# New durations for TensorE in the build-time account that orders a two-block transformer kernel

## The chip, the cores and the metric

The kernel runs on one core of one Trainium2 chip. The time is that of one execution on the device, in microseconds (us), from the first to the last instruction as the runs report it. The profile is of one such execution; its engines are called PE (TensorE, matrix products), PEld (its weight loads), DVE (VectorE), ACT (ScalarE), POOL (GpSimd) and SP (SyncE, which starts most transfers).

## The reference, cut to what matters

Two blocks of two layers each, over 256 tokens of width 1024, all in float32. The first block has a mixing layer with three kinds of heads and a SwiGLU; the second block has a gated linear recurrence (a), differential attention (b), a Fourier branch (c) and a merge of the three.

```
def _mixing(h, w_in, ...):                       # first block
    p = h @ w_in
    qa, ka, va, qi, ki, wi, qb, kb, vb, qc, kc, vc = split(p)
    qa, ka, qc, kc = rope(rms(.));  qi, ki = rope(.)
    oa = _dsa(qa, ka, va, qi, ki, wi)            # top 64 keys by an index score, then softmax
    ob = _stick_breaking(qb, kb, vb)             # cumulative sums over the keys
    oc = _swa_sinks(qc, kc, vc, sinks)           # band of 128 keys, softmax with sinks
    return rms(concat(oa, ob, oc), g_out) @ w_o

for l in range(2):
    sh1, sc1, g1, sh2, sc2, g2 = split(silu(c) @ w_mod[l] + b_mod[l])
    h = rms(x, ln1[l]) * (1 + sc1) + sh1
    x = x + g1 * _mixing(h, ...)
    h = rms(x, ln2[l]) * (1 + sc2) + sh2
    x = x + g2 * ((silu(h @ w_gate) * (h @ w_up)) @ w_down)

for l in range(2):                               # second block, with a context of 256 more tokens
    h = rmsnorm(x) * (1 + scale) + shift;  hc = rmsnorm(ctx) * (1 + scale_c) + shift_c
    aq, ak, av, ag, ao, az, bq, bk, bv, bz, cu, cz, mg = split(h @ w_in)     # and the same of hc
    y_a = rmsnorm(mlstm(aq, ak, av, ag)) * sigmoid(ao) * silu(az)
    y_b = rmsnorm(attend(bq, bk, bv, lam)) * silu(bz)
    y_c = real(fft2(cu)) * silu(cz)
    x = x + gate * (sum(sigmoid(mg_i) * (y_i @ w_i_out)) @ w_out)            # ctx likewise in layer 0
```

## The kernel before

All weights pass through SBUF once, in blocks of up to 8 x 128 rows and 256 columns. SP fetches a block into one of two buffers `raw`; ACT casts it to a float32r part `whi`, and DVE or POOL subtracts to get the rest `wlo`. The activations are split in the same way (`hhi` and `hlo`, or two planes of `h`). A dense product is three float32r matmuls per 128 rows (hi times hi, hi times lo, lo times hi): `mm3`, `dense_t` and `dense_n`. Some 24 of these 256-column matmuls make one group, and after each group the program calls `tick`.

Everything else is written between the groups. Each attention stage is a Python generator, an item of the class `Pipe`, that yields what its next piece reads. `tick` does four things: it may write one step of the modulations, a product of 32 rows by 512 columns over a fetched tile of weights `gw` (`fill`, `gemv`; such a step shows as x4 in the program's order and as x8 in the trace); it splits part of a weight block (`split_half`); it fetches (`ahead`); and it calls `Pipe.step`, which writes the next piece of each item that is ready. `drain` does the same without dense products until given items are finished. The weight blocks, gw tiles, PSUM banks and scratch tiles are rings, so that a piece that is written earlier also claims its buffers earlier.

What is ready is decided while the program is written, by `Clock`: an account of the time at which each engine gets to what it has been given. `Clock.run` starts an instruction at the latest of its engine's time, its inputs' and its ring's, and doubles a cost on PE where the account holds the clock to be low. `Engine.cost` gives the durations and `Engine.__getattr__` enters every instruction that the program writes; since it is also the helper that issues the real instruction, nearly every row of the trace has its line, L160. `Pipe.ready` lets a piece be written when its inputs' time is no later than PE's time in the account plus a slack; `fill_time`, `spare_time`, `ahead` and `split_half` compare with PE's time too. So the account sets the order in which each engine's queue is written, and nothing else: every engine works through its queue in that order, and waits are semaphores.

Names that the rows below show: `RC` are the rotated queries and keys of the c heads, `PC`, `PA` and `kk` projections, `aT` and `cT` their transposes, `S` scores, `nmax` the negative row maxima, `zB` and `eB` the stick-breaking logits and their sums, `rs` and `sst` a reciprocal root by three Newton steps on POOL; in the second block `M` and `wT` are masked weights of the recurrence and their transposes, `hA` its output, `rr` and `sh` its norm, `rsB` and `rtB` the norms of the b heads, `y` and `oB` normed head outputs. `stick`, `turned`, `attend` and `squares` in `mixing` write the first block's pieces; `tile_` and `out` in `a_items` and `b_items` the second's.

Of the kernel before, what the change touches and what calls it, by code (L numbers as in the profile page):

```python
# [7 lines left out]
F32 = mybir.dt.float32  # L8
# [17 lines left out]
EPS = 1e-6  # L26

# columns of w_in
QA, KA, VA, QI, KI, WI, QB, VB = 0, 256, 320, 384, 640, 704, 708, 1220
# columns of w_in_2  # L30
# [9 lines left out]
class Nothing:  # L40
    """stands for every object of a dry pass over the program"""
# [24 lines left out]
class Clock:  # L66
    """A rough account, while the program is written down, of when each engine gets to what it is given, in
    microseconds. Only the order in which independent work is written rests on it."""
# [20 lines left out]
    def cold(self):  # L89
        """whether the tensor engine's clock would slow down after this window of time"""  # L90
        return self.work.get(int(self.t["pe"] / 3.41), 0) < 3060

    def run(self, engine, outs, ins, cost, columns=0, delay=0.0):
        t = max([self.t[engine], self.ready(ins) + LAT] + [self.free.get(o.name, 0.0) + LAT for o in outs])
        if engine == "pe":
            w = int(t / 3.41)
            if self.work.get(w - 1, 0) < 3060:                      # the clock at half its rate
                cost *= 2
            self.work[w] = self.work.get(w, 0) + columns
# [15 lines left out]
def rows(aps):  # L115
    return aps[0].shape[0] / 128


class Engine:
# [3 lines left out]
    def cost(self, fn, out, ins, k):  # L123
        size = lambda ap: math.prod(ap.shape[1:])
        n = size(out)
        if self.name == "pe":
            if fn == "transpose":
                return 0.107, n * rows(ins)
            f = 1 if k["rhs"].dtype == F32R else 4
            c = max(0.107, n * f / 2400)  # L130
# [12 lines left out]
    def __getattr__(self, fn):  # L143
        real = getattr(self.real, fn)

        def call(*a, **k):
# [11 lines left out]
            else:  # L158
                self.clock.run(self.name, outs, aps, *self.cost(fn, outs[0], aps, k))
# [10 lines left out]
class Pool:  # L170
# [18 lines left out]
    def free(self, tag, bufs):  # L189
        """when the next place of a ring of tiles is free"""  # L190
# [9 lines left out]
def prm(ph):  # L200
    """the parameters of a phase: NAME_ph or NAME"""
# [8 lines left out]
class Pipe:  # L210
    """Work in stages beside the dense products. An item is a generator that yields what its next stage reads first. Each
    step writes the next stage of the items under way for which that is ready by the clock and starts new ones; of a
    group, limit items are under way at once."""
# [9 lines left out]
    def add(self, gen, after=(), group=None, limit=0, rank=5):  # L223
        """those of a lower rank come first"""
# [49 lines left out]
    def needed(self, items):  # L274
        """what has to run for items to finish"""
# [16 lines left out]
class Program:  # L292
    def __init__(self, tc, stack, args, out, order=None, upto=None):
# [8 lines left out]
        self.every, self.nticks = 0, 0         # a step of the modulations after every so many ticks  # L302
        self.pending = []
        self.nd = self.ns = self.nt = 0        # blocks fetched, split, taken
        self.hold = True                       # no blocks yet
        self.gd = self.gt = 0                  # rows for the modulations fetched, taken
# [18 lines left out]
    def any_ps(self):  # L325
        """a bank where nothing but dense products runs"""
# [9 lines left out]
    # =====================================================================================  # L336
    # Weights: blocks of up to 8 x 128 rows and 256 columns in the order of their use, fetched ahead and split
    # exactly into two float32r parts. A block: (rows of 128, ((tensor, layer, first row, first column, n), ...)).
    # The modulations' weights come apart from them, 128 rows at a time: (tensor, layer, first row, first column, n).
    # =====================================================================================  # L340
# [25 lines left out]
    def split_half(self, now=True):  # L366
        """splits one half of the next block's rows; False when there is nothing to do (if not now: nothing that has
        come by the clock)"""
# [24 lines left out]
    def ahead(self, g=0, n=0):  # L393
        """fetches what has a free place by the clock, and at least the first g rows and n blocks"""
# [21 lines left out]
    def drop(self, back=0):  # L416
        """the block taken last (or before) is used up"""
# [1621 lines left out]
```

## Time and profile before

| | |
|---|---|
| time, median of 3 runs | 2404.87 us (2397.66 to 2409.1) |
| profiled execution, span | 2406.6 us |
| PE busy | 2275.1 us, 95% of the span |
| DVE, ACT, POOL busy | 54%, 43%, 16% |
| mean granted clock of PE | 0.960 of full |
| bytes moved | 350.62 MB, mean 146 GB/s |

The profiled execution has no time of its own beside its span; the span lies 1.7 us above the median of the runs and inside their range. PE works through one queue in order, so time is lost where a piece at the head of that queue waits for another engine, and where PE runs at a lower granted clock. The program runs through the first block's layer 0 (mixing to about 210 us, SwiGLU to 440), its layer 1 (to 660 and 850), the second block's layer 0 (heads to 1320, merge to 1780) and layer 1 (heads to 2160, merge to the end).

### The profile page before, as it was taken

Reading aid. Unit: us, or ns where it says so; the run is one execution under the profiler, and the core shown is the slowest. Engines: PE = TensorE matmul, PEld = TensorE weight load, DVE = VectorE, ACT = ScalarE, POOL = GpSimd, SP = SyncE. Lnnn points to the kernel's source line nnn. Section 1 sums busy time; section 2 is a strip of 40 time slices with the busy share of each in tenths; the row PEclk is TensorE's granted clock in tenths of the full one; section 3 lists DMA queues with packets and bytes.
Section 4 is the critical chain, followed back from the end, with each engine's and each line's share of the span. In section 5 each row is a group of like instructions: output and inputs, shape, how many; then the busy total and the mean of one; then the engine's idle time right before and its main releaser. Section 6 shows DMA issues by size and latency. Waiting matters only on the chain. (4 is left out here: it accounts for less than half of the span.)

```text
span 2406.6 us, 39016 instructions
## 1 busy us (share of the span) xinstructions
PE 2275.1 (95%) x15672; PEld 2001.2 (83%) x15672; DVE 1298.5 (54%) x2556; ACT 1028.4 (43%) x1983; POOL 377.6 (16%) x901
## 2 busy tenths in 40 slices
PE   5988999898799999999799999999999999999999
PEld 2876889776689988888688888888897998889999
DVE  2745555675455546566564424435354665655665
ACT  2543435445344435555454323323254455544543
POOL 2321001452100001230232000000011332230000
PEclk8969999997899999999999999999999999999999
DMA  8727896652687542221222534433342322237765
GB/s 279 229 102 230 265 287 222 191 192 93 191 268 227 185 130 62 80 71 61 74 88 83 146 91 118 108 105 105 105 141 75 97 89 77 92 119 206 206 178 160
DMA packets 397142, 350.62 MB, mean 146 GB/s; under 512 B 12801, under 2 KB 366465, under 8 KB 396449
## 3 DMA queue, kind: packets, MB, share of 16 engines
q1 hardware_dynamic: 386752, 321.29, 44.2%
q0 software_dynamic: 8768, 23.76, 3.2%
q10 hardware_dynamic: 1440, 3.08, 0.4%
q8 instruction: 123, 2.02, 0.4%
q14 instruction: 59, 0.48, 0.1%
HBM read 335.50 MB, written 10.49 MB: 144 GB/s over the span
## 5 line engine op out<-in xcount | busy, mean ns | idle before, releaser
L160 DVE TENSOR_TENSOR wlo<-raw,whi 128x1024 fp32r<-128x1024 f32 (+1 forms) x465 | 548.7, 1213 | 439.7 <-ACT whi L160 438.6
L160 ACT CAST whi<-raw 128x1024 fp32r<-128x1024 f32 (+3 forms) x476 | 471.2, 1031 | 219.1 <-PE ps_mm L160 68.8
L160 PE MATMUL ps_mm<-whi,h 128*128 128x256 f32 x2304 | 442.2, 289 | 11.5 <-ACT h L160 4.5
L160 PEld LDWEIGHTS ps_mm<-whi,h 128*128 128x128 f32 x2304 | 364.2, 191 | 35.6 <-issue 17.6
L160 PE MATMUL ps_mm<-wlo,h 128*128 128x256 f32 x1152 | 324.1, 281 | 2.5 <-DVE wlo L160 2.5
L160 PE MATMUL ps_mm<-h,whi 128*128 128x512 f32 (+2 forms) x912 | 237.2, 349 | 0.0
L160 PEld LDWEIGHTS ps_mm<-wlo,h 128*128 128x128 f32 x1152 | 220.6, 191 | 6.6 <-DVE wlo L160 2.9
L160 PEld LDWEIGHTS ps_mm<-h,whi 128*128 128x128 f32 (+1 forms) x912 | 154.5, 185 | 32.6 <-issue 8.0
L160 PE MATMUL ps_mm<-h,wlo 128*128 128x512 f32 (+2 forms) x456 | 158.2, 347 | 0.0
L160 PE MATMUL ps_t<-h,whi 128*128 128x512 f32 (+1 forms) x592 | 147.9, 340 | 0.0
L160 PE MATMUL ps_s<-h,whi 128*128 128x256 f32 (+1 forms) x576 | 138.8, 332 | 0.0
L160 PE MATMUL ps_mm<-hhi,whi 128*128 128x256 f32 x416 | 124.5, 299 | 7.8 <-DVE xT L160 7.8
L160 PE MATMUL ps_mm<-hhi,wlo 128*128 128x256 f32 x416 | 120.9, 291 | 2.0 <-POOL wlo L160 2.0
L160 PE MATMUL ps_g<-gw,c 128*32 128x512 f32 (+1 forms) x640 | 97.4, 611 | 26.0 <-DMA gw<-in_w_mod_dram 18.6
L160 PE MATMUL ps_mm<-hlo,whi 128*128 128x256 f32 x416 | 121.0, 291 | 0.0
L160 PEld LDWEIGHTS ps_t<-h,whi 128*128 128x128 f32 x592 | 101.6, 188 | 12.6
L160 ACT ACTIVATE M<-ps_s,nmB,rsB 128x512 f32<-128x512 f32 (+1 forms) x96 | 67.0, 702 | 93.8 <-DVE nmB L160 93.8
L160 PEld LDWEIGHTS ps_s<-h,whi 128*128 128x128 f32 x576 | 97.5, 188 | 10.8
L160 PE MATMUL ps_t<-h,wlo 128*128 128x512 f32 (+1 forms) x296 | 100.8, 340 | 0.0
L160 PEld LDWEIGHTS ps_mm<-hhi,whi 128*128 128x128 f32 x416 | 83.0, 199 | 21.0 <-DVE xT L160 11.1
L160 PE MATMUL ps_s<-h,wlo 128*128 128x256 f32 (+1 forms) x288 | 96.0, 333 | 0.1
L160 PEld LDWEIGHTS ps_mm<-h,wlo 128*128 128x128 f32 (+1 forms) x456 | 84.5, 185 | 13.3 <-DVE wlo L160 0.2
(429 smaller groups left out, 5129.0 us busy)
## 6 DMA issues: line engine op xcount, KB each, us to landing
raw<-in_w_in_dram SPq DMA_DIRECT2D x72, 1024.0 KB, 5.2
raw<-in_w_in_dram SPq DMA_DIRECT2D x100, 512.0 KB, 4.2
gw<-in_w_mod_dram SPq DMA_DIRECT2D x96, 512.0 KB, 5.5
gw<-in_w_ada_dram SPq DMA_DIRECT2D x64, 384.0 KB, 5.4
raw<-in_w_gate_dram SPq DMA_DIRECT2D x44, 512.0 KB, 4.1
raw<-in_w_up_dram SPq DMA_DIRECT2D x44, 512.0 KB, 5.5
raw<-in_w_down_dram SPq DMA_DIRECT2D x16, 1024.0 KB, 5.0
raw<-in_w_out_dram SPq DMA_DIRECT2D x12, 1024.0 KB, 5.1
```

The costliest lines, as they stand in the source:

```text
L160: return real(*a, **k)
```

## The change

The costs of PE in the account change, and results of PE count as made 0.12 us after the engine is done with them. In `Engine.cost`, a transpose goes from 0.107 to 0.110 us; a float32r matmul of n columns from max(0.107, n/2400) to max(0.110, n/2400 + 0.014), which is 0.1207 in place of 0.107 for 256 columns and 0.2273 in place of 0.2133 for 512; a float32 matmul from max(0.107, 4n/2400) to two passes of max(0.107, n/1200) with 0.005 on top, three quarters of it where the operand has fewer than 128 rows. No instruction is added or taken away: PE has 15672 before and after.

```diff
@@ Engine.cost
         if self.name == "pe":
             if fn == "transpose":
-                return 0.107, n * rows(ins)
-            f = 1 if k["rhs"].dtype == F32R else 4
-            c = max(0.107, n * f / 2400)
+                return 0.110, n * rows(ins)
+            if k["rhs"].dtype == F32R:
+                return max(0.110, n / 2400 + 0.014), n * rows(ins)
+            c = 2 * max(0.107, n / 1200) + 0.005
+            if rows(ins) < 1:
+                c *= 0.75
             return (c / 3 if "tile_position" in k else c), n * rows(ins)
@@ Engine.__getattr__
-                self.clock.run(self.name, outs, aps, *self.cost(fn, outs[0], aps, k))
+                self.clock.run(self.name, outs, aps, *self.cost(fn, outs[0], aps, k), delay=0.12 if self.name == "pe" else 0.0)
...
```

The rest of the diff takes out comments. The helper's line is L163 in the changed kernel. Most of the order stays; what moves, moves by one group of 24 dense matmuls in most places. Three places follow. A row gives the line, the operation, out<-in, the size and how many stand together.

PE's queue at the end of the first block's layer 0 mixing, where the dense products of `w_in` have run out and `drain` writes the rest; before:

```order
L160 MATMUL ps_t<-ident,kk 128x128 x2
L160 MATMUL ps_g<-gw,c_88 32x512 x4
L160 MATMUL ps_t<-ident,RC 128x128 x2
L160 MATMUL ps_o<-PC,zB 128x64 x4
L160 MATMUL ps_t<-ident,PA 128x128 x4
L160 MATMUL ps_t<-ident,RC 128x128 x4
L160 MATMUL ps_s<-aT 128x256 x4
L160 MATMUL ps_s<-aT 128x128 x4
L160 MATMUL ps_t<-ident,RC 128x128 x4
L160 MATMUL ps_o<-PC,zB 128x64 x8
L160 MATMUL ps_t<-ident,S 128x128 x8
L160 MATMUL ps_s<-cT 128x256 x4
```

and the same place after:

```order
L163 MATMUL ps_t<-ident,kk 128x128 x2
L163 MATMUL ps_t<-ident,RC 128x128 x2
L163 MATMUL ps_t<-ident,PA 128x128 x4
L163 MATMUL ps_t<-ident,RC 128x128 x4
L163 MATMUL ps_o<-PC,zB 128x64 x12
L163 MATMUL ps_t<-ident,RC 128x128 x4
L163 MATMUL ps_s<-aT 128x256 x4
L163 MATMUL ps_s<-aT 128x128 x4
L163 MATMUL ps_s<-cT 128x256 x4
L163 MATMUL ps_t<-ident,S 128x128 x8
L163 MATMUL ps_g<-gw,c_88 32x512 x4
L163 MATMUL ps_o<-PA,S 128x64 x8
```

The modulation step behind `kk` has gone to a place behind the first eight transposes of `S`; all twelve products with `zB` and both groups of `RC` now stand ahead of the scores, and the first scores with `cT` ahead of the transposes of `S`. Further up, the stick-breaking scores and their sums are each written one group of 24 earlier; further down, the end of the stage holds four steps of the modulations (x4 + x4 + x8) where it held five.

PE's queue at the end of the a heads in the second block's layer 0 (each "..." is a group of 24 dense matmuls); before:

```order
L160 MATMUL ps_t<-ident,M_11533 128x128 x4
...
L160 MATMUL ps_o<-av,wT 128x256 x4
L160 MATMUL ps_t<-ident,M_11602 128x128 x2
L160 MATMUL ps_o<-av,wT 128x256 x2
L160 MATMUL ps_t<-ident,hA 128x128 x8
L160 MATMUL ps_mm<-whi_11741,h_6167 128x256
```

and after:

```order
L163 MATMUL ps_o<-av,wT 128x256 x4
L163 MATMUL ps_t<-ident,M_11581 128x128 x2
...
L163 MATMUL ps_o<-av,wT 128x256 x2
...
L163 MATMUL ps_t<-ident,hA 128x128 x8
L163 MATMUL ps_mm<-whi_11770,h_6167 128x256
```

The last pieces of the a heads stand one and two groups earlier, so 48 dense matmuls now lie between the last transposes of `M` and those of `hA`; the number of dense matmuls ahead of `hA` is the same. POOL's queue at this place keeps its order: two chains `rsB`, then `sh` and `rr`.

PE's queue at the end of the first block's layer 1 mixing; before:

```order
L160 MATMUL ps_o<-PA,S 128x64 x12
L160 MATMUL ps_g<-gw,c_88 32x512 x4
L160 MATMUL ps_t<-ident,PC 128x128 x8
L160 MATMUL ps_s<-eB,masks_253 128x256
...
L160 MATMUL ps_t<-ident,PA 128x128 x4
...
L160 MATMUL ps_g<-gw,c_88 32x512 x12
```

and after:

```order
L163 MATMUL ps_o<-PA,S 128x64 x12
L163 MATMUL ps_t<-ident,PC 128x128 x8
...
L163 MATMUL ps_s<-eB,masks_253 128x256
...
L163 MATMUL ps_t<-ident,PA 128x128 x4
...
L163 MATMUL ps_g<-gw,c_88 32x512 x16
```

The modulation step ahead of the transposes of `PC` is gone from there and stands as a fourth step at the end; the first "..." after is 12 dense matmuls that now lie between those transposes and the sums over `eB`. SP writes the first blocks of `w_gate` and `w_up` one step of the modulations earlier, behind four gw tiles in place of six.

## Rows read from the trace of the kernel before

**Rows 1.** Windows by stage: us, busy PE, PEld, DVE, ACT, POOL; granted clock, DMA

```profile
50.00:210.00 160.00, 147.48 (x968) 120.86 (x969) 90.58 (x247) 73.02 (x160) 42.89 (x83) 0.86 0.56 182
440.00:660.00 220.00, 185.94 (x1212) 154.16 (x1212) 123.47 (x313) 92.87 (x194) 77.75 (x116) 0.83 0.52 165
850.00:1320.00 470.00, 441.19 (x3170) 389.93 (x3169) 273.59 (x684) 227.59 (x572) 93.19 (x307) 0.97 0.25 78
1780.00:2160.00 380.00, 360.81 (x2679) 326.90 (x2678) 223.95 (x492) 184.03 (x394) 104.99 (x307) 0.98 0.32 97
```

**Rows 2.** Timeline, PE, end of layer 0's mixing: start, duration, operation [idle before <- releaser]

```profile
124.36 0.28 PE L160 MATMUL ps_mm<-wlo,hhi 128*128 128x256 f32 x1
124.48 0.28 PE L160 MATMUL ps_mm<-whi,hlo 128*128 128x256 f32 x1
...
126.61 1.00 PE L160 MATMUL ps_o<-PC,zB 128*128 128x64 f32 x8
...
132.76 1.12 PE L160 MATMUL ps_t<-ident,RC 128*128 128x128 f32 x4 [4.70 <-POOL RC L160]
...
137.72 1.52 PE L160 MATMUL ps_s<-aT 64*128 64x128 f32 x8 [1.83 <-DVE nmax L160]
...
174.17 1.94 PE L160 MATMUL ps_g<-gw,c 128*32 128x512 f32 x8
...
178.01 1.06 PE L160 MATMUL ps_g<-gw,c 128*32 128x512 f32 x8
...
185.50 1.05 PE L160 MATMUL ps_g<-gw,c 128*32 128x512 f32 x4 [1.86 <-DMA gw<-in_w_mod_dram]
```

**Rows 3.** Timeline, DVE and POOL, what the wait for RC comes from

```profile
111.66 1.02 DVE L160 SCALAR_TENSOR_TENSOR zB<-ps_s,zB 128x512 f32<-128x512 f32 x2 [1.34 <-PE ps_s L160]
...
119.75 0.21 POOL L160 TENSOR_SCALAR rs<-ss 128x16 int32<-128x16 int32 x1 [4.90 <-DVE ss L160]
...
131.44 1.26 POOL L160 TENSOR_TENSOR RC<-RC,rope_t 128x512 f32<-128x512 f32 x1
```

**Rows 4.** Window in that stage, columns as in rows 1

```profile
140.00:176.00 36.00, 36.00 (x144) 29.85 (x143) 9.84 (x49) 17.64 (x63) 0.00 (x0) 0.50 0.00 1
```

**Rows 5.** Timeline, PE and DVE, end of the first block's layer 1 mixing

```profile
575.65 1.94 PE L160 MATMUL ps_g<-gw,c 128*32 128x512 f32 x8
...
576.82 0.95 DVE L160 SCALAR_TENSOR_TENSOR eB<-zB,eB 128x768 f32<-128x768 f32 x1
...
580.67 1.11 PE L160 MATMUL ps_t<-ident,PC 128*128 128x128 f32 x4 [2.04 <-DVE hlo L160]
...
616.52 1.08 PE L160 MATMUL ps_g<-gw,c 128*32 128x512 f32 x4 [2.45 <-DMA gw<-in_w_mod_dram]
617.76 1.92 PE L160 MATMUL ps_g<-gw,c 128*32 128x512 f32 x4 [0.16 <-DMA gw<-in_w_mod_dram]
```

**Rows 6.** Timeline, POOL, DVE and PE, end of the a heads

```profile
1150.52 1.30 POOL L160 TENSOR_TENSOR rtB<-rsB 128x16 f32<-128x16 f32 x1
1150.52 2.37 DVE L160 TENSOR_TENSOR wlo<-raw,whi 128x1024 fp32r<-128x1024 f32 x2 [0.66 <-ACT whi L160]
1153.65 0.21 POOL L160 TENSOR_TENSOR rtB<-rsB 128x16 f32<-128x16 f32 x1
1159.66 0.20 POOL L160 TENSOR_TENSOR rr<-rr,rt 128x4 f32<-128x4 f32 x1
1160.40 2.03 PE L160 MATMUL ps_t<-ident,hA 128*128 128x128 f32 x8 [11.19 <-DVE hA L160]
```

**Rows 7.** Waits of PE, 1780 to 2160 us: total, times, longest

```profile
PE ps_mm L160 <- ACT whi L160: 3.2, 2, 1.9
PE ps_t L160 <- DVE y L160: 2.9, 5, 1.0
```

**Rows 8.** One round of the a heads: DVE makes M, PE transposes it

```profile
918.45 0.35 DVE L160 SCALAR_TENSOR_TENSOR M<-M,den,M 128x128 f32<-128x128 f32 x1
921.49 0.60 PE L160 MATMUL ps_t<-ident,M 128*128 128x128 f32 x4
```

## The prediction

> **What bounds the kernel now.** I read the windows by stage first, because PE's share of the whole says nothing about where its queue stands still. In [rows 1] the span less PE's busy time is 160 - 147.48 = 12.5 us in the first layer's mixing, 220 - 185.94 = 34.1 in the second's, 470 - 441.19 = 28.8 in the heads of the second block's layer 0 and 380 - 360.81 = 19.2 in those of its layer 1: 94.6 of the 131.5 us that PE is idle in all (2406.6 - 2275.1). The clock column says more of the first two: 0.86 and 0.83. So the kernel is bound by PE's queue, and what an order can give back lies in these four stages: waits at the head of the queue, and time at the lower clock. Then I read the timelines of the places where the two orders differ, asking at each which producer ends last.
>
> At the end of layer 0's mixing PE waits 4.70 us for POOL's RC and 1.83 for the maxima on DVE [rows 2]. Behind that it is busy all 36.00 of 36 us at a granted clock of 0.50, the lower of the two levels, 1.2 GHz [rows 4]. At the end of the a heads it waits 11.19 us for hA [rows 6], the longest wait of those stages.
>
> **The change, part by part.** Nothing is added or removed. The account now charges a group of 24 dense 256-column matmuls 24 x 0.1207 = 2.90 us in place of 24 x 0.107 = 2.57. In the trace their starts lie 124.48 - 124.36 = 0.12 us apart, or 24 x 0.12 = 2.88 [rows 2], so the account comes close. What follows is that inputs look ready fewer matmuls later: pieces move by whole groups, about 2.88 us of cover each, and modulation steps move where their turn falls.
>
> End of layer 0's mixing. (a) The stick-breaking scores and sums stand one group earlier. They feed DVE's zB, which feeds its next operations, then the sums of squares, POOL's root and POOL's RC: DVE waits 1.34 us for PE there, POOL 4.90 us for DVE's ss, and RC ends at 131.44 + 1.26 = 132.70 [rows 3], 0.06 before PE resumes. The bounds are 0 and -2.88; I take -1.3, the wait of DVE that goes away, since ahead of it DVE is at work. (b) All zB products and both groups of RC now stand ahead of the scores. The 1.83 us wait for the maxima is filled with that work: -1.83, with bounds 0 and -1.83. (c) The eight zB matmuls of 1.00 us lose their cover, since they ran before the wait on RC and now run behind it: +1.0. (d) The modulation step behind kk ran free, inside the same wait. Of the five steps, the one free step is gone, the two single ones in the tail are now both where PE is at the lower clock, so 2 x 1.94 in place of 1.94 + 1.06, or +0.88, and one goes to w_o, where dense work follows, at +1.06. (e) With the earlier steps sooner, their gw places come free sooner, and the last step's wait for its DMA goes: -1.86 (bounds 0 and -1.86). The sum for this stage is -1.3 - 1.83 + 1.0 + 0.88 + 1.06 - 1.86 = -2.05. What is late next is the softmax of the first group, for which the scores with cT are now the cover.
>
> End of layer 1's mixing [rows 5]. The step at 575.65 goes (-1.94). The wait of 2.04 us for hlo goes, because hlo is now written ahead of the work on eB on DVE, whose first operation started at 576.82; the sums over eB come late instead, by about the 0.95 us of such an operation, with twelve dense matmuls as cover: -2.04 + 0.95. The step comes back at the end as a fourth in a row that lives on DMA: the last one in the trace takes 617.76 + 1.92 - 616.52 = 3.16 us with its two tiles, beside a wait of 2.45 before it. SP also puts the first blocks of w_gate and w_up ahead of two of its tiles. So +3.16, with bounds 1.06 (a warm step) and 3.16 + 2.45 = 5.61. Sum +0.13, from -2.9 to +2.6.
>
> End of the a heads [rows 6]. Here 48 dense matmuls, 5.76 us, come between the last transposes of M and those of hA, and by the look of the order the 11.19 us wait should shrink by them. It can't by much: the same number of dense matmuls lies ahead of hA, and hA waits for rr, which ends at 1159.66 + 0.20 = 1159.86, 0.54 before PE resumes. POOL gets to rr only behind two chains rsB, whose place in POOL's queue does not move. They start when ACT and DVE have served the b heads, and ACT gets there sooner by what it no longer waits for the last pieces. Bounds: 0 and -5.76; I take -1.5, nearer to none, since the POOL chain stands. On POOL the same operation on rtB takes 1.30 us while DVE subtracts wlo with two SBUF inputs, and 0.21 when DVE rests. The Trainium skill, "GPSIMD Engine Reference", section 1 (Specifications), says that POOL shares its SBUF interfaces with DVE and contends with DVE instructions that read two SBUF inputs; the trace agrees, and by this rule work moved closer together would lengthen the chain by up to 1.30 - 0.21 = 1.1 us for each operation that it meets, so the term would be nearer 0 than -1.5.
>
> Layer 1 of the second block. The context's norm is written one group earlier, so that ACT's casts and h meet less of a wait; the start of the dense work waits for ACT 3.2 us in two places [rows 7]. DVE's y waits are 2.9 us in five, of which the oB pieces, now under dense work, are two. I take -1.0 for each, with bounds 0 and -3.2, 0 and -2.0. The other moves, within stages where PE has dense work to do, I cost at nothing: the dense work hides them, and the price if that cover is gone is the first rival.
>
> The sum: -2.05 + 0.13 - 1.5 - 1.0 - 1.0 = -5.4 us. The profiled execution would go from 2406.6 to 2401.2. It lies 1.7 above the median of the runs, so from 2404.87 it is 2399.5; I say 2399.
>
> **The rivals.** *Thinner cover (slower).* In the a heads each round's M is made on DVE and then transposed on PE. In the round of [rows 8] M ends at 918.45 + 0.35 = 918.80, and PE takes it at 921.49, 2.69 us later. Moved one group (2.88) earlier, PE would wait 0.19 there, and the full 2.88 in a round without slack. The program has 16 such rounds in each layer of the second block. If one in four of these 32 waits the full group, it costs 8 x 2.88 = 23, and the time is 2399.5 + 23 = 2422. For it: the account gives PE's results only 0.12 us of delay, and says nothing of late DVE or ACT. Against it: its new price of a group is that of the trace. It decides from about six full waits: 6 x 2.88 = 17.3, which is 12 more than the gain.
>
> *The tail warms up (faster).* In [rows 4] PE is busy 36 of 36 us at 0.50. If moving a modulation step to the front of the tail brings the clock to the upper level there, the work takes 18 us. ACT's 17.64 busy us in the same window then nearly fill it, so I count 14 of the 18, and the time is 2399.5 - 14 = 2385. The Trainium skill, "TensorE: Matmul & The Clock Gate", Part 1, says that the throttled state is the default and that activity releases it; by that rule alone a PE that is never idle would be warm in this window already. Here the trace disagrees, since the clock stays at 0.50 through 36 busy us. Against this rival: a step stands in the tail of the kernel before as well, at 174.17, and the clock rises only behind it, when the step at 178.01 takes 1.06 in place of 1.94 [rows 2]. For it: that it does rise there.
>
> *Nothing that ends last moves.* POOL's chains set both long waits. If they stand still, (a), the a heads' term and the small ones fall away, and gains and losses at the ends of the mixings cancel: 2405, within 1 us of before.
>
> **How the numbers follow.** Chances: the forecast 0.47, its own range 2387 to 2410 from the ends of its terms (low: -2.88 - 1.83 + 1.0 + 0.88 + 1.06 - 1.86 = -3.63 for layer 0, then -2.9 - 5.76 - 3.2 - 2.0, together -17.5; high: 1.0 + 0.88 + 1.06 = 2.94 for layer 0, then 2.6 and three times nothing, together +5.5); nothing moves 0.16; thinner cover 0.22; a warm tail 0.15. A measurement of this kernel tells about 0.5% from no change, 12 us, so faster means under 2392.8 and slower over 2416.9. Faster: 0.14 of the warm tail, 0.09 of the forecast and 0.01 more, 0.24. Slower: 0.18 of the thinner cover and 0.02 of the forecast, 0.20. The same: 0.56. The range that leaves out a tenth on either side runs from 2379, beyond the warm tail's 2385, to 2422, the price of the thin cover.
>
> **What would show each step.** Right: in the new trace the wait for POOL's RC begins earlier and PE resumes at about 131, no wait for nmax of over 1 us follows, and the wait for DMA at the last step of layer 0's mixing is gone; four steps end layer 1's mixing with DMA waits of some 5 us in all; hA is still waited for some 9 to 11 us, behind rr on POOL. Wrong: the wait for hA under 6 us, so that POOL's chain was not what held it; waits for M in the second block above 5 us in sum; a granted clock above 0.8 between 140 and 176. A change of over 12 us that lies outside these places would mean that the order matters where I took the dense work to hide it.

## The result, and the profile after

The changed kernel takes 2426.23 us (median of 4 runs, 2426.03 to 2429.84) against 2404.09 before (4 runs): 22 us slower, a ratio of 1.0097 with a 95% interval of 1.0069 to 1.0125. The forecast was 2399 with a range to 2422, so it was wrong in sign and outside its range. The rival "thinner cover" had named slower, and 2422.

To see where the time went, the two traces are laid side by side by the number of dense matmuls that PE has done, since these are the same in both kernels and in the same order. Stages are then cut at the same dense matmul, not at the same time. First, by these cuts, the kernel before: the first block's layer 0, then its layer 1 up to the second block's first dense products, then the heads of the second block's layer 0 and of its layer 1. The columns are those of [rows 1].

```profile
48.76:456.97 408.21, 382.66 (x2870) 331.40 (x2871) 229.54 (x474) 182.65 (x336) 66.88 (x109) 0.92 0.69 220
456.97:881.92 424.95, 395.75 (x2951) 353.10 (x2951) 231.72 (x465) 181.46 (x329) 82.70 (x133) 0.92 0.60 186
881.92:1328.37 446.45, 420.17 (x2975) 368.35 (x2974) 259.03 (x646) 216.28 (x550) 91.03 (x297) 0.98 0.25 79
1789.67:2156.12 366.45, 347.26 (x2563) 313.35 (x2562) 217.42 (x472) 177.49 (x381) 100.37 (x299) 0.98 0.30 92
```

The same four stages of the changed kernel:

```profile
48.38:456.83 408.45, 376.99 (x2871) 325.91 (x2871) 234.50 (x474) 181.98 (x336) 65.90 (x110) 0.93 0.69 219
456.83:884.54 427.71, 398.06 (x2950) 354.88 (x2951) 230.98 (x465) 181.26 (x329) 82.58 (x133) 0.91 0.60 185
884.54:1342.39 457.85, 425.03 (x2975) 372.89 (x2974) 259.20 (x647) 216.04 (x551) 93.27 (x297) 0.97 0.24 77
1804.00:2177.68 373.68, 349.12 (x2562) 315.79 (x2561) 217.64 (x472) 177.09 (x380) 97.79 (x300) 0.97 0.30 90
```

The first stage is level (+0.2), the second +2.8, the heads of the second block +11.4 and +7.2; the merge between them and the one at the end differ by 0.3 and less. What an execution adds by itself can be read from kernels in which PE's queue is the same: in the second stage the kernel before and the runs e1 and e6 of the experiments below take 424.95, 423.56 and 416.62 us, in the heads of layer 1 the kernel before and e4 take 366.45 and 370.05, and in those of layer 0, with nearly the same queue, the changed kernel and e9 take 457.85 and 453.66. So the +2.8 tells nothing, and the two heads' stages lie outside this spread. Span less busy time of PE gives its waits: in the two heads' stages they grow from 26.3 to 32.8 and from 19.2 to 24.6 us, together +11.9. The other 6.7 us of the 18.6 are PE busy for longer at a clock that is 0.97 in place of 0.98: behind some waits dense work runs at the lower level for a while, as two of the places below show. So the loss lies in the heads of the second block, as waits and as clock, and no one wait holds it. What PE waits for there, total, times and longest; in the changed kernel, 850 to 1345 us:

```profile
PE ps_t L163 <- DVE hA L163: 12.1, 1, 12.1
PE ps_s L163 <- ACT M L163: 4.7, 4, 2.7
PE ps_o L163 <- ACT ps_o L163: 3.4, 5, 0.8
PE ps_mm L163 <- DVE pq L163: 3.4, 5, 1.2
PE ps_t L163 <- DVE y L163: 3.3, 2, 2.2
...
PE ps_t L163 <- DVE M L163: 1.3, 2, 0.8
```

In the changed kernel, 1800 to 2190 us:

```profile
PE ps_t L163 <- DVE hA L163: 5.9, 2, 5.6
PE ps_t L163 <- DVE y L163: 4.6, 3, 2.2
PE ps_mm L163 <- DVE y L163: 3.5, 1, 3.5
```

In the kernel before, 850 to 1330 us, two of the same:

```profile
PE ps_mm L160 <- DVE pq L160: 1.7, 4, 0.7
PE ps_t L160 <- DVE y L160: 1.4, 3, 0.5
```

Against these and [rows 6, 7], hA in layer 0 went from 11.19 to 12.1, pq from 1.7 to 3.4 and y from 1.4 to 3.3 (pq are tiles of the Fourier branch); hA in layer 1 is new, and y there went from 2.9 to 4.6 + 3.5. The transposes of M, where the rival put its price, wait 1.3 us, and 1.8 before (the M of the row with ACT are weights of the b heads).

Three places show how a piece that is written earlier loses. The plainest is the first a head of layer 0 that ends. Before, on DVE and PE (starts, durations, waits):

```profile
978.68 1.28 DVE L160 TENSOR_TENSOR nat<-nat,rsB 128x512 f32<-128x512 f32 x2
980.62 1.14 DVE L160 TENSOR_SCALAR hA<-hA,rr 128x256 f32<-128x256 f32 x4 [0.66 <-POOL rr L160]
984.97 1.41 DVE L160 TENSOR_SCALAR y<-ps_t,ln_pk 128x512 f32<-128x512 f32 x2 [3.21 <-PE ps_t L160]
...
984.33 1.03 PE L160 MATMUL ps_t<-ident,hA 128*128 128x128 f32 x8
985.78 0.66 PE L160 MATMUL ps_t<-ident,nat 128*128 128x128 f32 x4 [0.41 <-DVE y L160]
```

and after, with a window of 10 us at the same place:

```profile
980.22 1.14 DVE L163 TENSOR_SCALAR hA<-hA,rr 128x256 f32<-128x256 f32 x4 [1.77 <-POOL rr L163]
981.27 1.29 DVE L163 TENSOR_TENSOR nat<-nat,rsB 128x512 f32<-128x512 f32 x2
982.48 1.22 DVE L163 TENSOR_TENSOR wlo<-raw,whi 128x1024 fp32r<-128x1024 f32 x1
983.61 1.40 DVE L163 TENSOR_SCALAR y<-ps_t,ln_pk 128x512 f32<-128x512 f32 x2
...
980.82 1.36 PE L163 MATMUL ps_t<-ident,hA 128*128 128x128 f32 x8
984.41 0.66 PE L163 MATMUL ps_t<-ident,nat 128*128 128x128 f32 x4 [2.23 <-DVE y L163]
...
980.00:990.00 10.00, 7.76 (x51) 7.09 (x51) 4.80 (x9) 1.32 (x4) 1.31 (x3) 0.83 0.50 155
```

The transposes of hA now come one group earlier, before DVE has done nat and wlo; y, which empties their PSUM bank, stands behind both, and PE waits 2.23 us for the bank where it waited 0.41. Then the clock falls: 0.83 in this window, where it was 1.00.

The second place is the a heads' end in layer 1. On POOL, before:

```profile
2037.79 0.24 POOL L160 TENSOR_SCALAR sh<-sh 128x2 f32<-128x2 f32 x1
...
2042.53 0.37 POOL L160 TENSOR_SCALAR ssB<-ssB 128x16 f32<-128x16 f32 x1
```

and after, on POOL and PE:

```profile
2059.33 0.71 POOL L163 TENSOR_SCALAR ssB<-ssB 128x16 f32<-128x16 f32 x1 [2.92 <-DVE ssB L163]
...
2064.89 0.19 POOL L163 TENSOR_SCALAR sh<-sh 128x2 f32<-128x2 f32 x1
...
2070.26 0.19 POOL L163 TENSOR_TENSOR rr<-rr,rt 128x2 f32<-128x2 f32 x1
...
2070.99 1.08 PE L163 MATMUL ps_t<-ident,hA 128*128 128x128 f32 x4 [5.65 <-DVE hA L163]
```

Two chains on POOL have changed places: the b heads' ssB is ahead of the norm of hA, and PE waits 5.65 us for hA where it had not waited. The third is the start of the b heads' scores in layer 0, after:

```profile
1189.12 1.12 PE L163 MATMUL ps_s<-xT,xT 64*128 64x512 f32 x2 [0.85 <-ACT M L163]
1191.46 0.58 PE L163 MATMUL ps_mm<-whi,h 128*128 128x256 f32 x1 [1.21 <-DVE pq L163]
...
1190.00:1200.00 10.00, 8.79 (x50) 8.05 (x50) 6.21 (x15) 4.41 (x11) 0.35 (x2) 0.66 0.33 105
```

The scores moved out of the dense stretch that had covered them, next to the short Fourier products. Two waits follow, and the next 24 dense matmuls begin at a clock that makes this window 0.66: from the first of them to the next piece it is 5.28 us (1191.46 to 1196.74), where it was 2.94 (1180.92 to 1183.86). Before, there was one wait of 0.66 us there and the clock was 1.00.

### The profile page after: what moved, and what is told of

The parts are those of the page before. It is cut to its first block, busy times and chain, and to the rows that moved or that the text cites. A ratio compares the mean times of both kernels' runs of the same rounds, so it can differ in the third digit from the quotient of the medians.

```text
span 2428.1 us, 39006 instructions
## 1 busy us (share of the span) xinstructions
PE 2278.9 (94%) x15672; PEld 2004.8 (83%) x15672; DVE 1302.4 (54%) x2556; ACT 1027.5 (42%) x1983; POOL 375.3 (15%) x901
## 5 line engine op out<-in xcount | busy, mean ns | idle before, releaser
L163 DVE TENSOR_TENSOR wlo<-raw,whi 128x1024 fp32r<-128x1024 f32 (+1 forms) x465 | 549.6, 1215 | 444.8 <-ACT whi L163 441.9
L163 ACT CAST whi<-raw 128x1024 fp32r<-128x1024 f32 (+3 forms) x476 | 471.1, 1031 | 224.7 <-PE ps_mm L163 77.0
L163 PE MATMUL ps_mm<-whi,h 128*128 128x256 f32 x2304 | 448.2, 291 | 8.4 <-ACT h L163 3.5
L163 PEld LDWEIGHTS ps_mm<-whi,h 128*128 128x128 f32 x2304 | 369.3, 194 | 30.5 <-issue 16.8
L163 PE MATMUL ps_mm<-wlo,h 128*128 128x256 f32 x1152 | 326.5, 283 | 0.9 <-DVE wlo L163 0.9
L163 PE MATMUL ps_mm<-h,whi 128*128 128x512 f32 (+2 forms) x912 | 237.3, 349 | 0.0
L163 PEld LDWEIGHTS ps_mm<-wlo,h 128*128 128x128 f32 x1152 | 223.2, 194 | 4.8 <-issue 2.4
L163 PEld LDWEIGHTS ps_mm<-h,whi 128*128 128x128 f32 (+1 forms) x912 | 154.3, 185 | 33.0 <-issue 8.3
L163 PE MATMUL ps_mm<-h,wlo 128*128 128x512 f32 (+2 forms) x456 | 158.0, 347 | 0.0
L163 PE MATMUL ps_t<-h,whi 128*128 128x512 f32 (+1 forms) x592 | 147.9, 340 | 0.0
L163 PE MATMUL ps_s<-h,whi 128*128 128x256 f32 (+1 forms) x576 | 138.9, 332 | 0.0
L163 PE MATMUL ps_mm<-hhi,whi 128*128 128x256 f32 x416 | 125.9, 303 | 7.3 <-DVE xT L163 7.3
L163 PE MATMUL ps_mm<-hlo,whi 128*128 128x256 f32 x416 | 122.2, 294 | 1.8 <-DVE hlo L163 1.8
L163 PE MATMUL ps_mm<-hhi,wlo 128*128 128x256 f32 x416 | 122.0, 293 | 2.0 <-POOL wlo L163 2.0
L163 PE MATMUL ps_g<-gw,c 128*32 128x512 f32 (+1 forms) x640 | 99.0, 627 | 24.6 <-DMA gw<-in_w_mod_dram 16.7
L163 PEld LDWEIGHTS ps_t<-h,whi 128*128 128x128 f32 x592 | 101.6, 188 | 12.6
L163 PEld LDWEIGHTS ps_s<-h,whi 128*128 128x128 f32 x576 | 97.5, 188 | 10.8
L163 ACT ACTIVATE M<-ps_s,nmB,rsB 128x512 f32<-128x512 f32 (+1 forms) x96 | 67.0, 702 | 92.5 <-DVE nmB L163 92.5
L163 PEld LDWEIGHTS ps_mm<-hhi,whi 128*128 128x128 f32 x416 | 84.2, 203 | 20.8 <-DVE xT L163 10.9
L163 PE MATMUL ps_t<-h,wlo 128*128 128x512 f32 (+1 forms) x296 | 100.7, 340 | 0.0
L163 PE MATMUL ps_s<-h,wlo 128*128 128x256 f32 (+1 forms) x288 | 95.8, 333 | 0.0
L163 PEld LDWEIGHTS ps_mm<-h,wlo 128*128 128x128 f32 (+1 forms) x456 | 84.5, 185 | 13.4 <-DVE wlo L163 0.2
```

What stands on the lines that cost most here:

```text
L163: return real(*a, **k)
```

## The experiments

All were timed beside the kernel before, on one chip for each group, and are compared with it there: its medians are 2407.39 us for e1 to e4, 2408.81 for e5 to e8, 2403.79 for e9 to e12 and 2406.08 for e13 and e14. Differences between stages are from one profiled execution of each. "Idle" below is span less PE's busy time in the heads of layer 0 and of layer 1, cut at the same dense matmuls as above: 26.3 and 19.2 before, 32.8 and 24.6 in the changed kernel.

**One part of the change alone.** Is it the price of dense matmuls, as the theory of thin cover has it?

```diff
# e1: of the change, only
+            if k["rhs"].dtype == F32R:
+                return max(0.110, n / 2400 + 0.014), n * rows(ins)
```

> Only the float32r price of the change (256 columns 0.107 to 0.1207, 512 columns 0.2133 to 0.2273); float32, transposes and the delay of results as before. Theory A (thin cover): the dearer dense group alone has the pieces written about a group earlier, in the second block above all, and without the delay of 0.12, which holds pieces back, they stand as early or earlier than in the changed kernel: 18 to 30 us slower than before (ratio 1.008 to 1.0125), with waits on DVE's y, M and hA and a lower clock behind them. Theory B (scatter: this order is a tuned one, and any account that shuffles it costs some 10 to 25 us): also 10 to 25 us slower. Theory C (the float32 and delay parts carry the loss): within 8 us of before.

Measured 2428.73 us, ratio 1.0105 (1.0081 to 1.013): the whole loss, in this part alone. Idle 37.6 and 25.4. The waits that theory A named are there: hA 12.1, y 5.2 and M 4.3 us in layer 0.

```diff
# e2: of the change, only (with the transposes' 0.110)
+            c = 2 * max(0.107, n / 1200) + 0.005
+            if rows(ins) < 1:
+                c *= 0.75
```

> Only the float32 and transpose prices of the change (float32 256 columns 0.427 to 0.432, three quarters of that on 64 rows; transposes 0.107 to 0.110); the float32r price and the delay as before. Theory A: pieces get cheaper on 64 rows, so the cover does not get thinner: within 8 us of before. Theory B: 10 to 25 us slower, as much as for any shuffle. Theory C: 8 to 20 us slower.

Measured 2396.39 us, ratio 0.9962 (0.9945 to 0.9979): faster, by 11 us, and so a little outside what theory A had said.

```diff
# e3: of the change, only
+ delay=0.12 if self.name == "pe" else 0.0
```

> Only the delay of 0.12 us before PE's results count as made; all prices as before. Theory A: the delay holds pieces back, so cover gets thicker where anything moves: within 8 us of before, rather faster. Theory B: 10 to 25 us slower. Theory C: up to 15 us slower.

Measured 2392.88 us, ratio 0.9952 (0.9932 to 0.9972): 14 us faster than before, more than any of the three theories had said; its ratio and that of e8 are the lowest of all.

```diff
# e5: the change without
-            if k["rhs"].dtype == F32R:
-                return max(0.110, n / 2400 + 0.014), n * rows(ins)
```

> The change without its float32r price: float32 and transpose prices and the delay of results as changed, 256 columns still 0.107. Theory A (the dearer dense group writes pieces too early, the rest is harmless): 8 to 25 us faster than before, since each of the two parts alone was 11 and 14 faster. Theory B (scatter: an order that differs is worth anything from -15 to +20 at random): between -15 and +20, with no sum of the two parts to be seen.

Measured 2399.52 us, ratio 0.9967 (0.9944 to 0.999): 9 us faster than before, which lies in the range of either theory, and no sum of e2 and e3. So the loss comes with the float32r price and is not there without it; the gains of the other two don't add, which is what theory B said of small shifts in order.

**More of it.**

```diff
# e11: the changed kernel with
-                return max(0.110, n / 2400 + 0.014), n * rows(ins)
+                return max(0.110, n / 2400 + 0.028), n * rows(ins)
```

> The changed kernel with twice the step in the float32r price (256 columns 0.1347 in place of 0.1207, 512 columns 0.2413). Theory A and A2 (the dearer PE is against DVE and ACT, the earlier pieces are written and the more they wait): 8 to 25 us slower than the changed kernel, 2434 to 2451, with more waits for DVE. Theory B (scatter around any change): no order between dose and time, 2395 to 2425 as likely as not.

Measured 2436.37 us, ratio 1.0141 (1.0115 to 1.0168): 10 us more than the change, in the order that dose and theory A give. Idle 35.3 and 24.3. But the 10 us are not in the heads: these take 458.44 and 377.19 us, 1.6 less together than with the single step of e1 (459.63 and 377.60), and the longer stage is the first, 414.10 us where the changed kernel has 408.45. So the order of the doses is not shown to come from thinner cover.

**Where.** A flag set with the phase of the program takes the old or the new prices.

```diff
# e4: all of the change in phases 0, 1 (first block); e6: in phases 2 to 5 (second block)
+            self.clock.new = ph in ('0', '1')
```

> The whole change in the account while the first block's two mixings and SwiGLUs up to the second block's first phase are written, the old account from there on. By the two traces the first block ends about level (dense products 2.4 us late at 621 us, and 0.5 to 3 late at 900). Theory A: within 6 us of before. Theory B: 5 to 15 us slower, its share of any shuffle.

Measured 2415.78 us, ratio 1.0038 (1.0018 to 1.0058): 8 us slower, a little more than theory A had it and within theory B's range. Its trace does not say where: its first two stages are 2.2 and 0.0 us longer than before, and the heads of layer 1, in which PE's queue is as before, 3.6.

> The old account while the first block is written, the whole change from the second block's first phase on. Theory A, by the two traces, in which the dense products fall behind by 10 us in the second block's layer 0 and by 7 in its layer 1: 10 to 18 us slower than before. Theory B: anywhere between -15 and +20.

Measured 2420.81 us, ratio 1.006 (1.0036 to 1.0084): 12 us slower, as expected. Idle 33.6 and 23.4. The halves make 8 + 12 = 20 of the 22, though by the stages above the first block holds only 3 of them.

```diff
# e10: the changed kernel, and in the phases of the second block's heads
+                if self.clock.heads:
+                    return max(0.107, n / 2400), n * rows(ins)
```

> The changed kernel, but with the old float32r price while the heads of both layers of the second block are written; float32 price, delay and everything else as changed. Theory A: half or more of the 22 us comes back, since these heads hold most of the new waits: 2402 to 2415. Rival (the loss is spread over all stages by the price): 2417 to 2426.

Measured 2414.2 us, ratio 1.0048 (1.0028 to 1.0068): 12 of the 22 come back. Idle 24.3 and 20.7. The heads' stage of layer 0, to be held against 457.85 and 446.45 above:

```profile
885.31:1327.21 441.90, 417.57 (x2975) 366.82 (x2974) 260.15 (x647) 216.41 (x551) 93.63 (x297) 0.98 0.24 80
```

**Is it that pieces come too early?** Two ways to write them later again, with the new price of PE left in.

```diff
# e7: the changed kernel, and
-        self.pipe.slack = p.SLACK
+        self.pipe.slack = p.SLACK - 0.4
```

> The whole change, and the slack with which a piece counts as ready lowered by 0.4 us in every phase (0.3 to -0.1, -1 to -1.4): about the 0.33 us by which a group of 24 got dearer. Theory A, in its form that a piece comes at most 0.33 us too early: most of the loss comes back, within 8 us of before. Rival A2 (the account of PE now runs ahead of those of DVE and ACT by 13 per cent of all dense time, and what it compares is off by many us, not 0.33): 15 to 25 slower, as the change. Theory B: anywhere.

Measured 2411.15 us, ratio 1.001 (0.9989 to 1.0031): no longer told apart from before. Idle 24.1 and 24.3, so layer 0's part is gone and layer 1's is not.

```diff
# e8: the changed kernel, and
-            return load + 0.05 + n / 1200 + ...      # ACT
+            return load + 0.08 + n / 1100 + ...
-        return 0.07 + n / 960 + ...                  # DVE
+        return 0.09 + n / 860 + ...
```

> The whole change, and the account's prices for DVE and ACT raised about as much as PE's (DVE 0.07 + n/960 to 0.09 + n/860, ACT 0.05 + n/1200 to 0.08 + n/1100, so that 512 columns go from 0.60 to 0.69 and from 0.48 to 0.55; the trace has 0.75 and 0.57 to 0.59). Theory A2 (the old cheap PE went with a cheap DVE and ACT, so that the ratio was right): the loss comes back, within 8 us of before or faster. Theory A: it comes back in part, 5 to 15 slower. Theory B: anywhere.

Measured 2396.91 us, ratio 0.9952 (0.9933 to 0.9971): the loss is gone and 12 us are gained over before. Idle 24.7 and 20.4. Both heads' stages, against the pairs above:

```profile
875.45:1318.70 443.25, 418.53 (x2975) 367.63 (x2974) 259.96 (x647) 216.72 (x550) 92.79 (x297) 0.98 0.24 80
1780.01:2149.79 369.78, 349.42 (x2563) 314.10 (x2562) 217.72 (x472) 177.06 (x381) 100.34 (x303) 0.97 0.30 92
```

Together they are level with before (813.0 us for 812.9), so what the price lost in the heads is gone; the gain lies elsewhere: the profiled execution is 8.8 us shorter than the one before, and 7.9 of that is in the first block.

```diff
# e14: the kernel before with e8's prices for DVE and ACT only
```

> The kernel before with only the account's prices for DVE and ACT raised as in e8, PE's as before. Theory A (later pieces are safer in general): 3 to 15 us faster than before, as e2, e3 and e8 were. Theory A2 (what counts is the ratio of PE's price to the others'): pieces now come too late, stages stretch into the drains, 5 to 20 slower than before.

Measured 2407.42 us, ratio 1.0008 (0.9988 to 1.0027): the same as before, which neither theory had said: A2, by which the ratio of the prices counts, wanted 5 to 20 us slower. Dearer PE alone loses, dearer DVE and ACT alone change nothing, both together gain.

**Do the longest waits carry it?** The root that hA waits for goes from POOL to DVE.

```diff
# e9: in out() of a_items, the changed kernel with
-            self.rsqrt(sh[:, t0:], rr[:, t0:], rt[:, t0:], nc.gpsimd)
+            self.rsqrt(sh[:, t0:], rr[:, t0:], rt[:, t0:], nc.vector if g == 3 else nc.gpsimd)
# e12: the same in e8; e13: as e9, and the operation ahead of it too
-            nc.gpsimd.tensor_scalar(sh[:, t0:], sh[:, t0:], 1.0 / 256, EPS, ...)
+            (nc.vector if g == 3 else nc.gpsimd).tensor_scalar(sh[:, t0:], ...)
```

> The changed kernel, and for the last a head of each layer of the second block the root rr (fourteen small operations) on DVE in place of POOL, where it stood behind the chains rsB; PE's order stays nearly that of the changed kernel. Theory P (the longest new waits are for hA, 5.65 us in layer 1 and 12.06 in layer 0, because pieces that were written sooner put POOL's rsB ahead of rr or leave it there, with less dense work behind to cover): the two waits shrink to 1 to 5 us together, 8 to 14 us faster than the changed kernel, 2412 to 2418. Rival (the waits are for other things in the same place: DVE is itself late there, with wlo ahead): under 4 us faster, 2423 to 2428.

Measured 2426.27 us, ratio 1.0102 (1.0076 to 1.0128): nothing. The run didn't test what it meant to: the operation on sh stayed on POOL behind both rsB chains, and hA was still waited for 10.88 us.

> The changed kernel with dearer DVE and ACT in the account, as in the run e8, and rr of the last a heads on DVE, as in e9. If both work as the theories say, the two add: the wait for hA that is left in e8 (6.86 us in layer 0) goes too: 2386 to 2393, faster than e8 by 4 to 10. If rr on DVE only moves the wait: 2395 to 2400.

Measured 2404.79 us, ratio 1.0001 (0.998 to 1.0022): 8 us slower than e8, in which the same step was left out, and 13 by the two ratios; a miss.

> The changed kernel with the whole root of the last a heads' norm, sh and rr, on DVE, so that nothing of it stands behind POOL's rsB. Theory P (these waits carry a good part of the loss): the wait for hA in layer 0 falls from 12.06 to under 7 and in layer 1 from 5.65 to under 3, and the time to 2414 to 2421. Rival Q (what follows waits instead, since the next stage's inputs are made by the same DVE, ACT and POOL work, whose end does not move): the wait shrinks, but others grow, and the time stays within 4 us of the changed kernel, 2422 to 2430.

Measured 2423.02 us, ratio 1.0058 (1.0036 to 1.008): 17 us slower than before, where the change was 22, with intervals that overlap. Its wait in layer 0:

```profile
1160.32 2.05 PE L163 MATMUL ps_t<-ident,hA 128*128 128x128 f32 x8 [7.36 <-DVE hA L163]
```

The wait fell from 12.06 to 7.36, and in layer 1 the one of 5.65 went, 10.4 us in all, but the two stages are only 2.5 and 1.1 us shorter than in the changed kernel (455.35 and 372.55 us): in layer 0 PE is idle 4.2 us less (28.6) and busy 1.7 us more. Rival Q was nearer. The longest waits show the loss; taking them away gave back about a third of their length, no more than executions of one order differ by.

**Do the pieces stand earlier where it loses?** The traces can be counted for this. For every PE instruction of a stage that is no dense matmul, take the number of dense matmuls ahead of it, and compare it with the kernel before. In the heads of layer 0 the changed kernel has 496 of 968 such instructions earlier and 18 later, on average 15 dense matmuls earlier; e1, e6, e9, e11 and e13 have 15 to 16, and in these six kernels the stage is 6 to 13 us longer than before. In e2, e5, e7, e8, e10, e12 and e14 they stand 7 to 9 later than before, and the stage is between 5 us shorter and 2 us longer. So earlier pieces go with the loss there, and later ones with its absence. e3 is the exception that limits this: its pieces stand 13 earlier and its stage is only 4 us longer, so it also matters which pieces they are. In layer 1 the six have their pieces 4 to 5 earlier and lose 6 to 11 us; but e12 and e14, where they stand 2 and 12 later, lose 10 there too, so pieces may also come too late.

## Why the prediction was wrong, point by point

The step that failed is the one that cost the other moves "within stages where PE has dense work to do" at nothing, because "the dense work hides them". The heads of the second block, where these moves lie beside the few that were forecast at -3.5 us together, got 11.4 + 7.2 = 18.6 us longer: that cover was what the new price had thinned. It is the prediction's own last sign, a change of over 12 us that lies, but for the waits for hA and y, outside the places that it names. The prediction argued that the new price of a group, 2.90 us, comes close to the 2.88 of the trace, and took that for a reason against the rival. It had read the 2.88 at one place, in the first block. In the heads of layer 0 of the kernel before, these two lie 21 dense matmuls apart:

```profile
1181.15 0.28 PE L160 MATMUL ps_mm<-wlo,h 128*128 128x256 f32 x1
...
1183.54 0.28 PE L160 MATMUL ps_mm<-wlo,h 128*128 128x256 f32 x1
```

That is 2.39/21 = 0.114 us each, or 2.73 for a group. Where the loss lies, the old price (2.57) was 6% low and the new one is 6% high. By the old one the account has PE at a place sooner than it gets there, so that pieces are held back; by the new one it has PE there later, and inputs look ready too soon, measured in dense groups. e1, e5, e10 and the count above show this much: the price alone loses 21, without it nothing is lost, with the old price in the heads half of it comes back, and the pieces of the heads stand earlier with it.

Whether the ratio to the other engines' prices is the reason, as theory A2 has it, is not shown. The account has 0.60 us for 512 columns on DVE (0.07 + 512/960) and 0.48 on ACT (0.05 + 512/1200). Read as PE's price is read, from one start to the next, plain operations take just that in the kernel before:

```profile
1148.59 1.28 DVE L160 TENSOR_REDUCE ssB<-M 128x8 f32<-128x512 f32 x2 [2.30 <-ACT M L160]
...
941.24 0.58 ACT L160 COPY wT<-ps_t 128x512 f32<-128x512 f32 x1
941.72 0.80 ACT L160 ACTIVATE M<-M,mn 128x256 f32<-128x256 f32 x2
```

The two reductions take 1.28 us together and one by itself 0.68, so 0.60 lie between their starts, and the copy is followed after 941.72 - 941.24 = 0.48. Others are dearer than the account has them: an exponential with its sum on ACT takes 0.77 (from 1008.12 to 1008.89), for 0.68. So the dearer DVE and ACT of e8 are in part a margin put back, as the lower slack of e7 is, and e14, the same margin without the new price, changed nothing.

The first block's layer 0. (a) POOL's chain came earlier by more than the -1.3 of the forecast: RC ends at 126.77 + 1.40 = 128.17, where it was 132.70. PE uses only half of that: the bank that the transposes of PA need waits for DVE, and RC is taken at 130.54 in place of 132.76. (b) failed: the wait for nmax did not go. (d, e) The last pair of steps runs without a wait for its DMA, as said. PE, at the end of this stage:

```profile
126.77 1.40 POOL L163 TENSOR_TENSOR RC<-RC,rope_t 128x512 f32<-128x512 f32 x1
...
130.04 0.66 PE L163 MATMUL ps_t<-ident,PA 128*128 128x128 f32 x4 [2.40 <-DVE mod L163]
130.54 0.60 PE L163 MATMUL ps_t<-ident,RC 128*128 128x128 f32 x4
...
137.91 1.73 PE L163 MATMUL ps_s<-aT 64*128 64x128 f32 x7 [1.96 <-DVE nmax L163]
...
177.98 2.80 PE L163 MATMUL ps_g<-gw,c 128*32 128x512 f32 x16
```

The dense products of w_o begin 4.1 us earlier than before (185.8 against 189.8), but their first 17 start 0.22 us apart where it was 0.13, and by 205 us the two kernels are level again (0.4 us apart), so the term of -2.05 came to nothing within its stage.

The first block's layer 1. The step at 575.65 is gone, and the wait for hlo is 0.81 in place of 2.04; but a second one of 1.83 follows behind the first seven dense matmuls, so that the -2.04 was not gained. The four steps at the end wait 2.43 and 0.83 for their tiles:

```profile
615.75 1.05 PE L163 MATMUL ps_g<-gw,c 128*32 128x512 f32 x4 [2.43 <-DMA gw<-in_w_mod_dram]
617.63 4.48 PE L163 MATMUL ps_g<-gw,c 128*32 128x512 f32 x12 [0.83 <-DMA gw<-in_w_mod_dram]
```

They end at 617.63 + 4.48 = 622.11, where it was 619.68: the end of the mixing is 2.4 us late, against +0.13 forecast with a bound of +2.6.

The a heads in layer 0. That POOL's chains hold hA, so that 48 dense matmuls of cover shift nothing, was right: PE waits 12.06 us, rr ends on POOL at 1164.77 + 0.20 = 1164.97, and PE resumes at 1165.51.

```profile
1164.77 0.20 POOL L163 TENSOR_TENSOR rr<-rr,rt 128x4 f32<-128x4 f32 x1
1165.51 2.02 PE L163 MATMUL ps_t<-ident,hA 128*128 128x128 f32 x8 [12.06 <-DVE hA L163]
```

From the a heads' pieces to the dense work behind hA the two kernels come 3.0 us closer (8.1 us apart at the dense matmul that starts at 1142.26 before, 5.1 at the one at 1162.08), twice the -1.5 of this term and within its bounds.

Layer 1 of the second block. The waits for ACT's casts that the prediction had shrink stayed (2.9 for 3.2 us), and y's grew from 2.9 to 8.1 in the rows of layer 1 above: -2.0 forecast, +7.2 measured in that stage.

Of the rivals, thinner cover gave the place (the second block's heads) and the kind of loss, but not what waits: rounds of M have 1.3 us there (4.3 in e1, with the price alone), and it is hA, y, pq and the b heads' scores. That its time (2422) comes near is luck, since it was the price of eight full waits for M. The tail did warm in the profiled run of the changed kernel: 0.74 where it was 0.50, but with 6.89 us idle in the same 36.

```profile
140.00:176.00 36.00, 29.11 (x156) 22.32 (x154) 15.08 (x73) 18.07 (x68) 0.00 (x0) 0.74 0.23 76
```

What stays open: whether a price of 0.114 in the heads would lose too, which no run tried; whether the new price acts in part through the account's guess of the clock, since `Clock.run` doubles costs by it; and why e2, e3, e5 and e8 are faster than the kernel before. For e3 its profiled run has most of it in the first stage, where the clock of the window shown last is 0.93; whether that follows from its order was not tried apart.

## What to carry to other kernels

A planner's account that orders work by "is it ready" compares the engines' times, so one engine's price moves pieces everywhere, also where dense work seems to hide them. A price read at one place (0.12 us) need not hold at another (0.114), and an old price that is too low can have been a margin: taking it away cost 22 us here, and another margin (a lower slack, or dearer DVE and ACT) took the loss back. When a change writes pieces one group earlier, ask for each what stands ahead of its producers in their own queues, and what frees the bank or ring place that it takes; a long wait that the trace names need not be the one whose removal pays. Test such a table by its parts: one price alone showed here what a reading of the order had not.

## What the runs showed of the hardware that was not expected

The tail of the first mixing has a clock that differs by order and by execution. In the kernel before, PE was busy 36.00 of 36 us at 0.50 [rows 4]; e6, whose first block is written as before, shows 36.00 and 0.50 again. In the same window of the run e3, where the order differs, it was

```profile
140.00:176.00 36.00, 33.13 (x218) 21.25 (x217) 19.31 (x88) 20.93 (x75) 0.00 (x0) 0.93 0.49 175
```

at 0.93, with PE less busy. e8 and e12, in which PE has the same order up to there, differ by themselves: 0.69 and 0.83. The Trainium skill, "TensorE: Matmul & The Clock Gate", Part 1, says that activity releases the throttle; the first of these rows disagrees, since 36 us of small matmuls without a pause did not release it. The spread between runs goes with the clock as well: of the kernel before's runs beside e1, the one of 2413.88 us had a mean granted clock of 0.956, the one of 2393.28 had 0.965.

In the second block a wait can cost more than itself. Behind waits of 0.85 and 1.21 us the window from 1190 to 1200 shows 0.66, and behind one of 2.23 the window from 980 to 990 shows 0.83, where the kernel before has 1.00 in both. Not every wait does this: around waits of 1.10 and 0.84 us the window from 1100 to 1110 of the kernel before shows 1.00. The Trainium skill, on the same page under "HAM oscillation", tells of waits for DMA behind which PE is throttled again and the next work starts cold; the trace agrees, though its waits are for DVE and ACT and shorter than those of the page's case.
